# A decoder layer whose MLP runs as seven block products: where the weight sums are made, how the stages meet, and how the last chunk is done

## The chip, the cores and the metric

The kernel runs on one core of a Trainium2 chip. The metric is the device time of one execution in microseconds. The core has five engines that run their own instruction streams in order: TensorE (PE in the profile, its weight loads PEld), VectorE (DVE), ScalarE (ACT), GpSimd (POOL) and SyncE (SP). SP issues most transfers; GpSimd issues the transfers that add into their destination.

## The reference

One decoder layer on 512 tokens of width 2048, in float32: three mixers side by side, an output projection, and an MLP, then a last normalisation.

```python
def hybrid_layer(x, ...):
    h = rmsnorm(x, norm1_w)
    proj = h @ w_in
    ...
    y = jnp.concatenate([y_sb.astype(x.dtype), y_sc, y_gdn], axis=-1)
    x = x + y @ w_out
    h2 = rmsnorm(x, norm2_w)
    return x + jnp.square(jax.nn.relu(h2 @ w_up)) @ w_down
...
return rmsnorm(x, final_norm_w)
```

The change touches the MLP alone: `w_up` is 2048 x 8192, `w_down` 8192 x 2048.

## The kernel before

Every float32 operand of a large product is **split** into two fp32r parts, a rounded high part (a cast on ScalarE, L824) and the rest (a subtraction on VectorE, L825). A product is then three matmuls on TensorE (`mm3`, L108 to L112): high times high, high times low, low times high.

The MLP multiplies 2 x 2 block matrices with seven products in place of eight, numbered 1 to 7. Each product has one combination of weight blocks on one side and one of activation blocks on the other. The weight blocks are written `src(kh, d)`, and a **quarter** is one block of 128 x 1024 float32 (512 KB). The weight sides are: product 1 (0,0); 2 (1,0); 5 (0,0)+(0,1); 6 that plus (1,1); 3 (1,1); 4 the sum of all four; 7 (1,1)+(0,1). They are done in the order 1, 2, 5, 6, 3, 4, 7 (`PROD`).

`w_prep` (L831) makes the weight side of one product. At product 1 it loads three quarters on SP: `t` = (0,0), `v` = (1,0), `u` = (1,1). At product 5 and at product 7 a transfer issued by GpSimd adds (0,1) into `t` and into `u` (L835). At products 6 and 4 VectorE adds `u` and `v` into `t` (L836). Then the quarter is split into a tile `W`, of which there are three, used in turn: the split for a product can begin when the product three places before it is done with its tile. The quarters come from one ring of eight tiles.

Stages of the MLP, in the order of the program:

- **Up** (`up_pair`, L875): 32 groups. A group is seven products of 24 matmuls of 128 x 256 each, into PSUM tiles `pu`; 168 matmuls. ScalarE copies finished products out (L893), VectorE combines them (L897), applies relu and the norm factor (L920), ScalarE squares (L921), VectorE forms the activation sums for the next stage (L734, L738), and SP stores the 1 MB result `hs` to memory.
- **Down** (`unit`, L970): eight blocks (b) of two halves (j). One pair (b, j) is seven products of two chunks with 12 matmuls of 128 x 512 each, into `pp`; 168 matmuls. Activation tiles `A1` to `A7` are loaded from `hs` (`ha`) and split once per block. VectorE adds each product into the residual `xq` (L963, L966).
- The **last block** is cut: for both halves only half of its depth goes through the seven products, 84 matmuls each. The other half of its depth, for all columns, is done by plain products (`last`, L1032): 16 sums of 12 matmuls, 192 in all, after their weights `Wl` and activations `hl` have been split. Between them GpSimd multiplies by the final norm's weights (L1041).

Between the output projection (L767 to L794, 16 products of 48 matmuls over the tiles `big`) and the up stage lies a seam: the `mlp` pool with `q` and `W` takes over the memory of `big`. Group 0 there does products 1 and 2 up to their last step, and then the turn of the last block and the norm factor (`ending`). Between up and down lies another: the `A` tiles take over the memory of the up stage's activations.

Loads and splits carry a priority (`DPRIO`, `APRIO`): the scheduler puts them ahead of the code they are written in, some products early. That decides each engine's order.

## Time and profile before

| | us |
|---|---|
| median of 3 runs | 2417.95 (2413.97 to 2422.53) |
| the profiled execution | 2417.65 |
| its span in the trace | 2415.9 |

| stretch of the trace, us | what runs there |
|---|---|
| 0 to 912 | mixers and output projection |
| 912 to 932 | seam, with products 1 and 2 of group 0 |
| 932 to 1745 | the rest of the up stage |
| 1748 to 2357 | down stage by seven products |
| 2357 to 2408 | plain products of the last block |
| 2408 to 2416 | last norm and store |

The page's first part gives each engine's busy time. A row of a window gives, for one stretch, its length, the busy time of each engine with the number of instructions that began in it, the granted clock of TensorE, the share of the DMA engines' time in use and the rate. A row of the timeline has start, length, engine, line, operation, tile written and tiles read, a count if several are merged, and in brackets the idle time before it with what ended it. A row of the waits has who waited for whom, the total, the number of times and the longest. Up to 912 us the order of instructions on every engine is the same in both kernels, so the profile there holds for both.

### The profile page before, as it was taken

What the parts mean: (1) busy time and instruction counts of PE and PEld (TensorE: products, weight loads), DVE (VectorE), ACT (ScalarE), POOL (GpSimd) and SP (SyncE); (2) the same over time, 40 slices, a digit from 0 to 9 for tenths busy, and PEclk for the clock granted to TensorE, in tenths of its full rate; (3) what the DMA queues carried; (4) which work ended last, traced back from release to release, by engine and by line L of the source; (5) the groups of instructions that cost most, each with busy time, mean ns of one, the idle gap of its engine ahead of it and who ended that gap; (6) DMA issues with size and microseconds to landing.
All of it is one profiled execution on the core that took longest, in us unless ns stands there. A gap on an engine that the chain in (4) does not pass through costs nothing.

```text
span 2415.9 us, 33083 instructions
## 1 busy us (share of the span) xinstructions
PE 2245.7 (93%) x12698; PEld 1942.2 (80%) x12698; DVE 1656.8 (69%) x2320; ACT 1045.8 (43%) x1630; POOL 177.4 (7%) x235
## 2 busy tenths in 40 slices
PE   9999999999999998888888888988899999999987
PEld 8887787888888887888888788888777878777866
DVE  5799898646576555555555555565688988898875
ACT  5746554334445443333333333333344444444434
POOL 0000000000000110000000000000001010000003
PEclk9999999999999998999999999999999999999999
DMA  5322222232223445555555546555687675767542
GB/s 186 97 91 87 65 87 85 82 93 77 81 84 112 154 129 169 152 136 150 150 128 155 150 132 157 140 141 149 169 269 206 174 196 150 202 177 194 139 117 93
DMA packets 153582, 332.49 MB, mean 138 GB/s; under 512 B 19312, under 2 KB 60400, under 8 KB 153424
## 3 DMA queue, kind: packets, MB, share of 16 engines
q1 hardware_dynamic: 135568, 265.37, 32.6%
q0 software_dynamic: 17856, 65.02, 16.3%
q8 instruction: 99, 1.62, 0.3%
q14 instruction: 59, 0.48, 0.1%
HBM read 284.85 MB, written 45.48 MB: 137 GB/s over the span
## 4 chain that ended last, share of the span: by engine, by line
issue 55%; PE 34%; DVE 4%; POOL 2%; DMA 2%; ACT 1%; SPq 0%; POOLq 0%; ACTq 0%; DVEq 0%
PE mm L110 9%; PE mm L111 9%; PE mm L112 9%; POOL q L835 2%; DVE Yq L439 1%; PE mm L275 1%; PE mm L273 1%; PE mm L274 1%; DVE wlo L105 1%; DVE tq L437 1%; DMA q<-in_wd_dram 1%; DMA tmp<-x 0%; PE v L200 0%; PE v L201 0%; DVE W L825 0%
## 5 line engine op out<-in xcount | busy, mean ns | idle before, releaser
L824 ACT CAST W<-q 128x1024 fp32r<-128x1024 f32 x434 | 443.3, 1048 | 846.0 <-DMA q<-in_wu_dram 356.0
L825 DVE TENSOR_TENSOR W<-q,W 128x1024 fp32r<-128x1024 f32 x434 | 520.6, 1222 | 341.3 <-ACT W L824 340.4
L110 PE MATMUL mm<-big,whi 128*128 128x512 f32 x1024 | 406.1, 397 | 1.8 <-DVE tmp L558 1.6
L112 PE MATMUL mm<-big,wlo 128*128 128x512 f32 x1024 | 404.9, 396 | 0.0
L111 PE MATMUL mm<-big,whi 128*128 128x512 f32 x1024 | 404.8, 395 | 0.0
L110 PE MATMUL pu<-XS,W 128*128 128x256 f32 x1024 | 307.9, 301 | 62.6 <-ACT W L824 61.3
L110 PE MATMUL pp<-W,A 128*128 128x512 f32 x840 | 329.2, 395 | 16.3 <-ACT W L824 12.6
L112 PE MATMUL pu<-XS,W 128*128 128x256 f32 x1024 | 307.8, 301 | 36.2 <-DVE W L825 36.2
L111 PE MATMUL pp<-W,A 128*128 128x512 f32 x840 | 332.1, 395 | 5.0 <-DVE W L825 4.5
L112 PE MATMUL pp<-W,A 128*128 128x512 f32 x840 | 329.7, 393 | 1.0 <-DVE A L825 0.8
L111 PE MATMUL pu<-XS,W 128*128 128x256 f32 x1024 | 300.0, 293 | 0.0
L105 DVE TENSOR_TENSOR wlo<-raw,whi 128x512 fp32r<-128x512 f32 (+1 forms) x288 | 193.9, 675 | 147.0 <-ACT whi L104 133.3
L104 ACT CAST whi<-raw 128x512 fp32r<-128x512 f32 (+1 forms) x288 | 174.1, 606 | 267.0 <-PE mm L111 227.1
L110 PEld LDWEIGHTS pu<-XS,W 128*128 128x128 f32 x1024 | 205.7, 201 | 77.0 <-ACT W L824 76.4
L112 PEld LDWEIGHTS pu<-XS,W 128*128 128x128 f32 x1024 | 206.5, 202 | 46.7 <-DVE W L825 46.2
L110 PEld LDWEIGHTS mm<-big,whi 128*128 128x128 f32 x1024 | 193.9, 189 | 40.5 <-DVE tmp L558 1.8
L112 PEld LDWEIGHTS mm<-big,wlo 128*128 128x128 f32 x1024 | 193.8, 189 | 39.6
L111 PEld LDWEIGHTS mm<-big,whi 128*128 128x128 f32 x1024 | 193.7, 189 | 38.9 <-DVE big L723 0.3
L111 PEld LDWEIGHTS pu<-XS,W 128*128 128x128 f32 x1024 | 205.7, 201 | 0.0
L110 PEld LDWEIGHTS pp<-W,A 128*128 128x128 f32 x840 | 159.1, 189 | 57.3 <-ACT W L824 20.5
L111 PEld LDWEIGHTS pp<-W,A 128*128 128x128 f32 x840 | 159.1, 189 | 46.5 <-DVE W L825 12.3
L112 PEld LDWEIGHTS pp<-W,A 128*128 128x128 f32 x840 | 159.1, 189 | 34.2 <-DVE A L825 2.1
(289 smaller groups left out, 3459.5 us busy)
## 6 DMA issues: line engine op xcount, KB each, us to landing
q<-in_wd_dram SPq DMA_DIRECT2D x98, 512.0 KB
raw<-in_wa_dram SPq DMA_DIRECT2D x192, 256.0 KB
q<-in_wu_dram SPq DMA_DIRECT2D x96, 512.0 KB
q<-in_wu_dram POOLq DMA_DIRECT2D x64, 512.0 KB, 7.2
hs<-h SPq DMA_DIRECT2D x32, 1024.0 KB
q<-in_wd_dram POOLq DMA_DIRECT2D x60, 512.0 KB, 7.8
ha<-hs SPq DMA_DIRECT2D x49, 512.0 KB
raw<-in_wo_dram SPq DMA_DIRECT2D x64, 256.0 KB
```

The lines of the kernel that those rows point to most:

```text
L104: S.copy(out=hi[:, :n], in_=raw[:, :n])
L105: V.tensor_tensor(out=lo[:, :n], in0=raw[:, :n], in1=hi[:, :n].bitcast(F32), op=ALU.subtract)
L110: PE.matmul(p, lhsT=lh, rhs=rh, start=first, stop=False, skip_group_check=more)
L111: PE.matmul(p, lhsT=lh, rhs=rl, start=False, stop=False, skip_group_check=more)
L112: PE.matmul(p, lhsT=ll, rhs=rh, start=False, stop=last, skip_group_check=more)
L273: PE.matmul(o, lhsT=xw[k][:, 0, s], rhs=hi[:, ws], start=k == 0 and b % 2 == 0, stop=False)
L274: PE.matmul(o, lhsT=xw[k][:, 0, s], rhs=lo[:, ws], start=False, stop=False)
L275: PE.matmul(o, lhsT=xw[k][:, 1, s], rhs=hi[:, ws], start=False, stop=k == KT - 1 and b % 2 == 1)
L437: V.tensor_tensor(out=tv, in0=B[:, 0:i, i:i + 1].broadcast_to([16, i, n]), in1=Y[:, i:i + 1, i:32].broadcast_to([16, i, n]), op=ALU.mult)
L824: S.copy(out=o[:, 0], in_=src)
L825: V.tensor_tensor(out=o[:, 1], in0=src, in1=o[:, 0].bitcast(F32), op=ALU.subtract)
L835: more = lambda t, kh, d: nc.gpsimd.dma_start(out=t, in_=src(kh, d), accum_op=ALU.add)
```

## The change

It does these things:

1. All four quarters of a product set are loaded on SP: `t` (0,0), `v` (1,0), `x` (0,1), `u` (1,1), each from a ring of its own (three tiles for `t`, two for the others; nine tiles where there were eight).
2. Product 5's sum is made on VectorE from `x`. Straight after it, GpSimd begins a transfer that adds (1,1) into `x`; the result is the weight side of product 7.
3. In the up stage VectorE makes the sums of products 5, 6 and 4, and one adding transfer a group is left. In the down stage the order is 1, 2, 5, 6, 3, 7, 4 (`DOWN`); VectorE makes the sums of 5 and 6, and after the split for 6 a transfer adds (1,0) into `t` for product 4. Two adding transfers a chunk are left, as before.
4. Group 0's products 1 and 2 take their weights through the small tiles `whi` and `wlo` that served the output projection (`wload`), and six tiles of the `mlp` pool are allocated first (`ahead`).
5. `A1` of block 0 is loaded and split during the last up group, in tiles of the `mlp` pool.
6. The last block does half j = 0 in full by the seven products (168 matmuls) and half j = 1 in full by plain products (192 matmuls). The plain weights come through the same quarters; half of them are split into `W`, half into the tiles of `A5`, `A6`, `A3` and `A7`. The norm's work for half 0 lies beside the first 96 plain matmuls.

The number of matmuls in each stage stays the same.

```diff
-    PROD = (1, 2, 5, 6, 3, 4, 7)
+    UP = (1, 2, 5, 6, 3, 4, 7)
+    DOWN = (1, 2, 5, 6, 3, 7, 4)
...
+    def q_tile(tag):
+        return mlp.tile([P, 1024], F32, name="q", tag="q" + tag, bufs=3 if tag == "t" else 2)
+
+    def quarter(src, tag="t"):
+        q = ahead.pop(tag, None) or q_tile(tag)
         nc.sync.dma_start(out=q, in_=src)
         return q
...
+    def w_prep(n, st, src, down, split_too=True):
         with tc.high_priority(DPRIO):
-            more = lambda t, kh, d: nc.gpsimd.dma_start(out=t, in_=src(kh, d), accum_op=ALU.add)
-            more_on_v = lambda t, u: V.tensor_tensor(out=t, in0=t, in1=u, op=ALU.add)
+            on_v = lambda t, u: V.tensor_tensor(out=t, in0=t, in1=u, op=ALU.add)
             if n == 1:
-                st["t"] = quarter(src(0, 0))
-                st["v"] = quarter(src(1, 0))
-                st["u"] = quarter(src(1, 1))
+                for q, d in (("t", (0, 0)), ("v", (1, 0)), ("x", (0, 1)), ("u", (1, 1))):
+                    st[q] = quarter(src(*d), q)
             elif n == 5:
-                more(st["t"], 0, 1)
+                on_v(st["t"], st["x"])
+                nc.gpsimd.dma_start(out=st["x"], in_=src(1, 1), accum_op=ALU.add)
             elif n == 6:
-                more_on_v(st["t"], st["u"])
-            elif n == 4:
-                more_on_v(st["t"], st["v"])
-            elif n == 7:
-                more(st["u"], 0, 1)
-            o = mlp.tile([P, 2, 1024], F32R, name="W", tag="W", bufs=3, align_bytes=256)
-            split(o, st[{2: "v", 3: "u", 7: "u"}.get(n, "t")])
+                on_v(st["t"], st["u"])
+            elif n == 4 and not down:
+                on_v(st["t"], st["v"])
+            if not split_too:
+                return
+            o = ahead.pop("W", None) or w_tile()
+            split(o, st[{2: "v", 3: "u", 7: "x"}.get(n, "t")])
+            if n == 6 and down:
+                nc.gpsimd.dma_start(out=st["t"], in_=src(1, 0), accum_op=ALU.add)
...
+            Ws[n] = w_prep(n, st, lambda kh, d: wu[g, kh, d], False, g > 0 or n not in (1, 2))
+            if g == 0 and n in (1, 2):
+                Ws[n] = [wload(wu[0, n - 1, 0][:, 512 * c:512 * c + 512], 512) for c in range(2)]
...
     for g in range(FF // P // 2):
+        if g == FF // P // 2 - 1:
+            a_prep(0, 1, None)
         up_pair(g)
...
-        for j in range(2):
+        for j in range(2 if b < ND - 1 else 1):
...
+    def plain(c, d, kh):
+        q = quarter(wd[ND - 1, 1, kh, d][:, 1024 * c:1024 * (c + 1)], "txvu"[2 * d + kh])
+        if c == 0:
+            o = w_tile()
+        else:
+            n = (5, 6, 3, 7)[2 * d + kh]
+            o = dp.tile([P, 2, 1024], F32R, name=f"A{n}", tag=f"A{n}", bufs=1, align_bytes=256)
+        split(o, q)
+        return o
```

**VectorE in the up stage, around the start of a group.** Before, with `q_11518` as the group's `t`, `q_11520` its `v`, `q_11522` its `u`; `W_11524`, `W_11554`, `W_11584` belong to products 1, 2 and 5:

```order
L825 TENSOR_TENSOR W_11524<-q_11518,W_11524 128x1024
L825 TENSOR_TENSOR W_11554<-q_11520,W_11554 128x1024
L897 TENSOR_TENSOR raw_11289<-pu_11300,tmp_11474 128x256
L897 TENSOR_TENSOR raw_11290<-pu_11300,tmp_11385 128x256
L920 SCALAR_TENSOR_TENSOR raw_11289<-raw_11289,Rb_7222 128x512
L920 SCALAR_TENSOR_TENSOR raw_11290<-raw_11290,Rb_7222 128x512
L825 TENSOR_TENSOR W_11584<-q_11518,W_11584 128x1024
```

After, on the same engine at the same place, with `q_11560` as `t`, `q_11562` as `v`, `q_11564` as `x`; `W_11568`, `W_11598`, `W_11629` belong to products 1, 2 and 5:

```order
L825 TENSOR_TENSOR W_11568<-q_11560,W_11568 128x1024
L842 TENSOR_TENSOR q_11560<-q_11560,q_11564 128x1024
L825 TENSOR_TENSOR W_11598<-q_11562,W_11598 128x1024
L915 TENSOR_TENSOR raw_11329<-pu_11342,tmp_11517 128x256
L915 TENSOR_TENSOR raw_11330<-pu_11342,tmp_11428 128x256
L940 SCALAR_TENSOR_TENSOR raw_11329<-raw_11329,Rb_7222 128x512
L940 SCALAR_TENSOR_TENSOR raw_11330<-raw_11330,Rb_7222 128x512
L825 TENSOR_TENSOR W_11629<-q_11560,W_11629 128x1024
```

Product 5's sum stands on VectorE directly behind the split for product 1, and the adding transfer into `x` can begin from there.

**TensorE at the start of the up stage.** Before, the first matmuls behind the output projection (`W_8763` and `W_8788` are the split weights of products 1 and 2):

```order
L110 MATMUL pu_8766<-XP_7204,W_8763 128x256
L111 MATMUL pu_8766<-XP_7204,W_8763 128x256
L110 MATMUL pu_8791<-XP_7204,W_8788 128x256
L111 MATMUL pu_8791<-XP_7204,W_8788 128x256
L763 MATMUL pu_8823<-ident_78,tmp_8717 128x128 x4
L112 MATMUL pu_8766<-XP_7204,W_8763 128x256
```

After, at the same place (`whi` and `wlo` are the small tiles):

```order
L109 MATMUL pu_8779<-XP_7204,whi_8769 128x256
L110 MATMUL pu_8779<-XP_7204,whi_8769 128x256
L111 MATMUL pu_8779<-XP_7204,wlo_8770 128x256
L109 MATMUL pu_8779<-XP_7205,whi_8769 128x256
L110 MATMUL pu_8779<-XP_7205,whi_8769 128x256
L111 MATMUL pu_8779<-XP_7205,wlo_8770 128x256
```

Products 1 and 2 no longer read the `W` tiles, and the turn (L763) has moved behind all 48 of their matmuls.

**ScalarE at the end of the last block's seven products.** Before, the last two casts of `W` and what follows them (`hl` and `Wl` are the plain products' operands):

```order
L824 CAST W_19971<-q_19879 128x1024
L824 CAST W_19988<-q_19883 128x1024
L824 CAST hl_20011<-tmp_20009 128x512
L824 CAST hl_20016<-tmp_20014 128x512
L824 CAST hl_20021<-tmp_20019 128x512
L824 CAST hl_20026<-tmp_20024 128x512
L824 CAST Wl_20035<-q_20033 128x512
```

After (`W_20104` and `W_20119` are the two chunks of product 4, the last of the seven; `W_20146` and `W_20151` are the first plain weights; `A3_20312`, `A6_20307`, `A5_20302` and `A7_20317` are those of the second 96 plain matmuls):

```order
L824 CAST W_20104<-q_19860 128x1024
L824 CAST A3_20312<-q_20310 128x1024
L824 CAST A6_20307<-q_20305 128x1024
L824 CAST W_20119<-q_19883 128x1024
L824 CAST A5_20302<-q_20300 128x1024
L824 CAST W_20146<-q_20144 128x1024
L824 CAST A7_20317<-q_20315 128x1024
L824 CAST W_20151<-q_20149 128x1024
```

Three casts of weights that are used last now stand ahead of the last chunk of product 4 and of the first plain weights.

More of the change, by code (lines that the diff above doesn't have):

```diff
@@ L854, in h_tile @@
         return mlp.tile([P, 8, HT], F32, name="h", tag="h", bufs=2)
+    ahead = {}
+    for n in ("t", "v", "h", "W", "x", "u"):
+        ahead[n] = {"h": h_tile, "W": w_tile}.get(n, lambda: q_tile(n))()
     X4 = []
@@ L983, in unit @@
                     s = slice(i * P, (i + 1) * P)
[L984 to L985 removed]
+                    mm3(p[:, i], A[:, 0, k, s], A[:, 1, k, s], w[:, 0], w[:, 1], new and k == 0, k == HK - 1, not new)
+        for h, d in {1: ((0, 0),), 5: ((1, 1),), 6: ((0, 1),), 7: ((1, 0),)}.get(n, ()):
             x_load(h, d, j)
@@ L1009, in trunk @@
-    hl = []
-    for k in range(FBLK):
-        kh, sl = k // 2, HK // 2 + k % 2
-        t = tmp()
-        nc.sync.dma_start(out=t.rearrange("p (i t) -> p i t", i=2), in_=hs[ND - 1][:, 2 * kh:2 * kh + 2, sl])
-        o = fin.tile([P, 2, T], F32R, name="hl", tag="hl", bufs=FBLK, align_bytes=256)
-        split(o, t)
-        hl.append(o)
-    wfc = [fin.tile([P, 2, 512], F32, name=f"wf{d}") for d in range(2)]
-    for d in range(2):
-        nc.sync.dma_start(out=wfc[d], in_=wf[:, d * 1024:(d + 1) * 1024].rearrange("p (j f) -> p j f", j=2))
@@ L1020, in trunk @@
-    Wl = {}
-    for j in range(2):
-        for d in range(2):
-            for kh in range(2):
-                q = quarter(wd[ND - 1, j, kh, d][:, 1024:2048])
-                for k in range(2):
-                    o = fin.tile([P, 2, 512], F32R, name="Wl", tag="Wl", bufs=12, align_bytes=256)
-                    split(o, q[:, k * 512:(k + 1) * 512])
-                    Wl[j, d, kh * 2 + k] = o
+            for n in DOWN:
+                unit(b, j, n, dst)
+    with tc.high_priority(APRIO):
+        a_prep(ND - 1, 21, dp)
@@ L1045, in trunk @@
             for i in range(2):
-                last(0, d, h, i)
+                last(0, Wd, d, h, i)
+                norm_part(d, 0, h, i)
+    for d in range(2):
+        for kh in range(2):
+            Wd[d, kh] = plain(1, d, kh)
     for h in range(2):
```

85 lines of the change are left out of this document (48 added, 37 removed).

## The prediction

> **What bounds the kernel now.** I read the engines' busy times first, then the windows of the stretches that the change touches.
>
> ```profile
> span 2415.9 us, 33083 instructions
> PE 2245.7 (93%) x12698; PEld 1942.2 (80%) x12698; DVE 1656.8 (69%) x2320; ACT 1045.8 (43%) x1630; POOL 177.4 (7%) x235
> ...
> 912.40:931.55 19.15, 10.32 (x55) 9.20 (x55) 7.22 (x10) 7.73 (x11) 2.44 (x2) 0.73 0.90 304
> 931.55:1744.73 813.18, 703.05 (x5328) 672.36 (x5328) 467.06 (x603) 293.08 (x416) 56.51 (x65) 0.96 0.55 145
> 1748.44:2356.70 608.26, 589.72 (x2521) 474.22 (x2522) 514.59 (x452) 266.59 (x267) 50.46 (x58) 0.99 0.67 183
> 2356.70:2407.78 51.08, 45.75 (x192) 36.70 (x191) 29.05 (x46) 24.15 (x57) 19.16 (x15) 0.97 0.20 77
> ```
>
> TensorE is busy 93% of the span, but the records of its matmuls overlap, so the number to use is the stride between two starts. It comes from stretches without a wait:
>
> ```profile
> 1302.06 0.28 PE L111 MATMUL pu<-wlo,W 128*128 128x256 f32 x1
> 1304.34 0.28 PE L112 MATMUL pu<-whi,W 128*128 128x256 f32 x1
> ...
> 2106.29 0.39 PE L112 MATMUL pp<-W,A 128*128 128x512 f32 x1
> 2117.85 0.39 PE L112 MATMUL pp<-W,A 128*128 128x512 f32 x1
> ```
>
> In the up stage 19 strides take 2.28 us, 0.120 each; with a second stretch at 0.118 I use **0.1195**. In the down stage 51 strides take 11.56 us, **0.2267**. Without waits, then, the rest of the up stage would take 5328 x 0.1195 = 636.7 us where it takes 813.2: 176.5 us are lost, 5.5 in each of 32 groups. The down stage would take 2520 x 0.2267 = 571.3 where it takes 608.3, and the plain products 192 x 0.2267 = 43.5 where they take 51.1. The up stage is the place to look at. Its waits and one group show what ends last:
>
> ```profile
> POOL q L835 <- DVE W L825: 770.1, 65, 17.2
> ACT W L824 <- DMA q<-in_wu_dram: 356.0, 59, 8.0
> ...
> L824 ACT CAST W<-q x206: 1038/1054/1060, 1754.8 to 2345.3; 128x1024 fp32r<-128x1024 f32 x103
> L825 DVE TENSOR_TENSOR W<-q,W x206: 1214/1220/1227, 1756.1 to 2346.4; 128x1024 fp32r<-128x1024 f32 x103
> ...
> 1297.52 0.86 POOL L835 DMA_DIRECT2D q<-in_wu_dram  x1 [13.68 <-DVE W L825]
> 1305.04 2.94 ACT L824 CAST W<-q 128x1024 fp32r<-128x1024 f32 x3 [5.38 <-DMA q<-in_wu_dram]
> 1306.12 3.50 DVE L825 TENSOR_TENSOR W<-q,W 128x1024 fp32r<-128x1024 f32 x3 [3.83 <-ACT W L824]
> 1306.14 0.38 PE L110 MATMUL pu<-XS,W 128*128 128x256 f32 x1 [1.52 <-ACT W L824]
> 1307.73 0.42 PE L110 MATMUL pu<-XS,W 128*128 128x256 f32 x1
> 1310.51 0.41 PE L111 MATMUL pu<-XS,W 128*128 128x256 f32 x1
> 1310.92 0.28 PE L110 MATMUL pu<-XS,W 128*128 128x256 f32 x1
> ```
>
> GpSimd waits for a split to be done with a quarter, begins the adding transfer at 1297.5, ScalarE waits until 1305.0 for it to land, casts, and TensorE, which ran out of products 1.52 us before, starts at 1306.1. It then runs slow until 1310.9: at 1307.7 the stride is some 0.21, so about 16 matmuls lose 1.5 us more. The chain is issue 0.9, landing 7, cast 1.05, and ahead of it a split that waits for a tile of `W`. It runs twice a group, for products 5 and 7. Products that cost 24 x 0.1195 = 2.87 us each don't cover it.
>
> **The change, part by part.**
>
> *Up stage.* Product 5's sum goes to VectorE: 1.22 us, once in 32 groups, 39 us more; the adding transfer for it goes (32), a load on SP comes (32). With two tiles for `x` that load is begun a group ahead, about 20 us. The other transfer now starts behind product 5's sum, which stands right behind the split for 1. That split can begin when product 3 is done: cast 1.05, split 1.22, sum 1.22, issue 0.86, landing 7.2 make 11.6 us. Its result is first wanted by the cast for product 7, whose tile comes free when product 6 ends, six products or 17.2 us after product 3. So 5.6 us are left; at the longest landing of the stage some 0:
>
> ```profile
>   DMA to landing us min/median/max: 5.4/7.2/12.9
> ```
>
> What is late next? VectorE: 467.06 us in 5328/168 = 31.7 groups, 14.7 a group, with the sum 15.9 of 20.1. ScalarE: 293.08/31.7 = 9.2. DMA: a group now uses 0.55 x 25.4 = 14 us; by the queues
>
> ```profile
> q1 hardware_dynamic: 135568, 265.37, 32.6%
> q0 software_dynamic: 17856, 65.02, 16.3%
> ```
>
> a MB costs 0.163 x 2415.9/65.02 = 6.06 us as an adding transfer and 2.97 as a load, so half a MB moved from one to the other makes 14 - 3.0 + 1.5 = 12.5 of 20.1. Nothing is above 80%, so TensorE sets the end: 20.1 us a group, plus 0.2 a group for an odd late split (bounds 0 and 2.0, the latter a wait of 0.6 with the slow stretch of 1.5 behind it, once a group; I take nearly the lower since the smallest reserve that I find by following VectorE's order through a group at these durations is 1.9 us). 636.7 + 6 - 813.2 = **-170.5**.
>
> *The first seam.*
>
> ```profile
> 912.49 0.69 DVE L776 TENSOR_TENSOR tmp<-mm,xr 128x512 f32<-128x512 f32 x1 [7.67 <-PE mm L112]
> 917.70 1.23 DVE L731 TENSOR_TENSOR XS<-xsum,XS 128x1024 fp32r<-128x1024 f32 x1 [1.11 <-ACT XS L730]
> 918.67 0.58 PE L110 MATMUL pu<-XP,W 128*128 128x256 f32 x1 [6.27 <-ACT W L824]
> 931.55 0.39 PE L110 MATMUL pu<-XS,W 128*128 128x256 f32 x1 [2.41 <-ACT W L824]
> ```
>
> TensorE stops at 912.4 for 6.27 us, since `q` and `W` lie where `big` lay and are loaded and split only then; product 5 starts at 931.55. Now products 1 and 2 read small tiles that don't wait for `big`: 42 matmuls run from 912.4 on, 5 us. Product 5 needs `XS`, which ends at 918.9, the turn, and its own sum, cast and first split, about 2.6: 921.5. If the loads, which still can't start before `big` is free, land at 913 + 8, it is 913 + 8 + 1.2 + 1.05 + 1.2 = 924.5 or later. Bounds 918.9 and 926; I take the nearer row, `XS`: **-10**.
>
> *The second seam.*
>
> ```profile
> 1741.22 1.37 SPq L958 DMA_DIRECT2D ha<-hs  x3
> 1744.45 0.28 PE L112 MATMUL pu<-XS,W 128*128 128x256 f32 x1
> 1748.44 0.80 PE L110 MATMUL pp<-W,A 128*128 128x512 f32 x1 [3.71 <-ACT A L824]
> ```
>
> `A1` is loaded while the last group still runs, so the wait of 3.7 for its cast goes; a second of restart and `A2`'s load stay: I take 2 (0 to 3.7). **-1.7**.
>
> *Down stage.* Product 5's sum moves to VectorE, product 4's moves to a transfer: still four additions a pair there, still four adding transfers, and two more loads of 512 KB, 3 us of DMA time in 38. Late casts after transfers cost TensorE 37 us in 15 pairs' worth of products. Two changes cut this: product 5 needs no transfer, and product 4, now last, leaves its transfer product 3 and product 7 (2 x 5.44 = 10.9 us) to land in. But VectorE stands at 514.6/608.3 = 85%, at 88 to 90% when the stage is denser, and DMA goes from 0.67 to about 0.77. Each chunk's transfer frees `t` late: with three tiles, its next load has about a chunk, 2.7 us, to spare. I leave half a microsecond in each of 15 pairs, 8 us (bounds 0 and all of the 37). At the end of block 7 three casts of late plain weights stand ahead of the last chunk of product 4; their quarters wait for tiles, so ScalarE may stand in front of them for about 2 us and TensorE with it, near the row of the same place now:
>
> ```profile
> 2326.42 0.49 PE L110 MATMUL pp<-W,A 128*128 128x512 f32 x1 [2.18 <-ACT W L824]
> ```
>
> With the slow stretch I price it at 4. 571.3 + 8 + 4 - 608.3 = **-25.0**.
>
> *Plain products.* Now they start behind a wait of 5 us for the split of `Wl`:
>
> ```profile
> 2362.14 0.77 PE L111 MATMUL mm<-Wl,hl 128*128 128x512 f32 x1 [5.00 <-DVE Wl L825]
> ...
> 2374.51 1.29 POOL L1041 TENSOR_TENSOR xq<-xq,wf 128x512 f32<-128x512 f32 x1 [1.74 <-ACT tmp L1040]
> 2374.97 1.38 DVE L825 TENSOR_TENSOR Wl<-q,Wl 128x512 fp32r<-128x512 f32 x1 [0.44 <-ACT Wl L824]
> ```
>
> The activations are split already in the changed kernel, and its first weights use tiles of `W` that turn over during product 4. 43.5 + 1 - 51.1 = **-6.6** (bounds 0 and -7.6). The last norm, 8.1 us, stays. The row of 1.38 us is a split beside a product on GpSimd, where the operation of the same size at 912.49 took 0.69; the eight products for half 0 now lie beside splits as well, 8 x 0.7 = 5.6 us of VectorE in 23 us of matmuls, which hides them. The Trainium skill ("SBUF — State Buffer", section "Who interferes with whom") has a rule on it: a VectorE operation with two inputs in SBUF contends with a GpSimd instruction that reads SBUF, and the later one is held up. The doubled row agrees; by it the longest delay of one split is GpSimd's 1.29 us, which would cost up to 1.3 us where the first plain weights wait, and nothing in the sum is changed by it.
>
> **The sum.** -10 - 170.5 - 1.7 - 25.0 - 6.6 = -213.8, against the execution that was profiled, 2417.65 us (the span of 2415.9 and 1.75 around it): **2204 us**. The median shown, 2417.95, differs by 0.3. Less than 0.3%, 7 us, can't be told from no change here.
>
> **The rivals.**
>
> *A new wait in the up stage (A).* The splits come in one order on two engines that don't look ahead; a late cast for any of seven products would stop TensorE once a group, 0.6 of wait and 1.5 of slow stretch. For it: the shortest reserve is 1.9 us, and landings reach 12.9. Against: loads are begun 20 us ahead. 32 x 2 = 64: **2268**.
>
> *The down stage stays as bound as now (B).* VectorE at nearly 90% and DMA at 0.77 delay a load per chunk: all 25 us but a few stay, plus a cost of the third `t`'s late load. +28: **2232**.
>
> *The slow stretches stay (C).* The granted clock of the up stage is 0.96, and what I call slow restarts may come from something else than the waits; 32 x 1.5 = 48 then stay: **2252**. The Trainium skill speaks for it ("TensorE: Matmul & The Clock Gate", section "Why this matters for your kernels"): only idle gaps above about 3 us bring the clock down, so gaps of 1.52 wouldn't be the cause. The trace differs: a slow stretch stands right behind the gap of 1.52, and the long stretch 1850 to 2250 of the down stage, whose gaps are at most 0.8, has a clock of 1.00:
>
> ```profile
> 1850.00:2250.00 400.00, 394.47 (x1716) 320.02 (x1716) 347.17 (x302) 181.40 (x179) 36.54 (x42) 1.00 0.67 179
> ...
> PE pp L110 <- ACT W L824: 4.1, 8, 0.8
> ```
>
> *It doesn't do what it says (D).* If another chain in the up stage is as long as the one that goes, only the other terms are left, 43 us: **2374**. Against it: every wait of TensorE there is for a `W` that an adding transfer feeds.
>
> *Slower (E).* Product 5's sum now stands on VectorE at the head of everything else: behind it the split for 2, the taking of products, relu and the split for 5. If the load of `x` is late, all of this stops, and TensorE with it. The gain, 213.8/32 = 6.7 us a group, is used up when TensorE waits that long in each, that is when a load begun 20.1 us ahead, with the reserve of 1.9, takes some 29 us. The longest landing of an adding transfer is 12.9, at a DMA share of 0.55, and the first seam ran at 0.90. At 8 us late a group, 32 x 8 - 214 = +42: **2460**.
>
> **How the numbers follow.** Forecast 0.76, A 0.10, B 0.08, C 0.02, D 0.02, E 0.02. The forecast's own bounds are 2183 (no loss left in the up and down stages but the 4 at its end, the first seam at 918.9, nothing at the second) and about 2217 (seam at 926, the 8 in the down stage doubled). The range 2183 to 2268 takes in A, B and C and leaves D and E out. Faster by over 0.3%: all but E, with a little for what I don't see, 0.97; within 0.01; slower 0.02.
>
> **What would show it.** In the changed kernel: groups of the up stage 20.1 to 20.5 us apart at a granted clock of 1.00, ScalarE's wait for `in_wu` transfers nearly gone (the step on the chain); else A, with TensorE waiting for a `W` whose quarter came from SP. Product 5 of group 0 at 919 to 926. No wait for `A` at the second seam. VectorE at 88 to 90% in the down stage and TensorE's strides at 38.5 us a pair; a wait at product 4's last chunk and the first plain weights of 2 us. The prediction is wrong if landings of `x` grow past 17 us in the up stage, or if VectorE, not TensorE, turns out to be the engine that is waited for.

## The result, and the profile after

| | before | changed |
|---|---|---|
| median, us | 2417.95 | 2195.19 (2192.34 to 2196.6) |
| the profiled execution's span, us | 2415.9 | 2193.2 |
| ratio, 95% interval | | 0.9075 (0.906 to 0.9091) |

The kernel is 222.8 us faster; 213.8 were forecast. The page of the changed kernel, its first part and the two largest groups of its fifth (count, busy time and mean of one, then the idle time ahead of them and what ended most of it):

```profile
span 2193.2 us, 33146 instructions
PE 2153.2 (98%) x12698; PEld 1893.1 (86%) x12698; DVE 1695.1 (77%) x2335; ACT 1067.3 (49%) x1621; POOL 150.4 (7%) x203
...
L824 ACT CAST W<-q 128x1024 fp32r<-128x1024 f32 x436 | 455.0, 1051 | 563.4 <-PE pp L111 247.1
L825 DVE TENSOR_TENSOR W<-q,W 128x1024 fp32r<-128x1024 f32 x436 | 530.5, 1225 | 121.6 <-ACT W L824 121.0
```

What ended most of ScalarE's waits ahead of a cast of `W` was a transfer (356 us, in the up stage); over the whole changed kernel it is TensorE, at the tiles `pp` of the down stage (247 of 563 us). In the up stage, between 950 and 1550 us, its waits ahead of a cast are these (who waited for whom, total, times, longest):

```profile
ACT W L824 <- DVE q L842: 89.5, 60, 2.1
ACT W L824 <- issue: 87.3, 61, 1.5
ACT W L824 <- PE pu L111: 70.9, 60, 2.0
```

No transfer is among the first five. Casts now wait for VectorE's sums or for a tile that TensorE still reads, and since TensorE is busy throughout, these waits cost nothing. The same stretches as before, by the windows of the changed kernel (length, busy time of each engine, granted clock, DMA share, rate), from the last matmul of the output projection on:

```profile
907.34:916.34 9.00, 7.46 (x56) 6.41 (x54) 6.62 (x10) 5.25 (x9) 1.95 (x2) 1.00 0.68 229
916.34:1555.37 639.03, 635.55 (x5329) 634.53 (x5329) 510.51 (x636) 313.97 (x419) 28.32 (x33) 1.00 0.65 188
1555.37:2138.61 583.24, 575.54 (x2523) 473.24 (x2521) 518.59 (x453) 279.80 (x276) 55.14 (x61) 1.00 0.76 222
2138.61:2184.72 46.11, 44.26 (x193) 35.62 (x191) 22.67 (x31) 16.47 (x40) 16.14 (x13) 1.00 0.15 57
```

Beside the stretches of before, each from the first matmul of one to the first of the next:

| stretch | before, us | changed, us | difference | forecast |
|---|---|---|---|---|
| up to the end of the output projection | 912.2 | 907.3 | -4.9 | 0 |
| seam, to the first matmul of product 5 | 19.3 | 9.0 | -10.3 | -10 |
| up stage and second seam | 816.9 | 639.0 | -177.9 | -172.2 |
| down stage | 608.1 | 583.2 | -24.9 | -25.0 |
| plain products and end | 59.4 | 54.6 | -4.8 | -6.6 |

The first row is no effect of the change: the order of instructions there is the same, and of the kernels below, e1, with the seam of before, starts its last matmul of the projection at 906.85 and e9, with the changed seam, at 911.56. Executions differ there by some 5 us.

### The profile page after: what moved, and what is told of

It reads as the page before. It is cut to its first block, busy times and chain, and to the rows that moved or that the text cites. A ratio compares the mean times of both kernels' runs of the same rounds, so it can differ in the third digit from the quotient of the medians.

```text
span 2193.2 us, 33146 instructions
## 1 busy us (share of the span) xinstructions
PE 2153.2 (98%) x12698; PEld 1893.1 (86%) x12698; DVE 1695.1 (77%) x2335; ACT 1067.3 (49%) x1621; POOL 150.4 (7%) x203
## 3 DMA queue, kind: packets, MB, share of 16 engines
q8 instruction: 99, 1.62, 0.3%
## 4 chain that ended last, share of the span: by engine, by line
PE 91%; DVE 5%; DMA 1%; ACT 1%; issue 1%; SPq 0%; ACTq 0%; DVEq 0%
PE mm L110 10%; PE mm L109 10%; PE mm L111 10%; PE pu L111 10%; PE pu L109 10%; PE pu L110 10%; PE pp L110 8%; PE pp L111 8%; PE pp L109 8%; DVE wlo L104 1%; PE mm L274 1%; PE mm L272 1%; PE mm L273 1%; DVE W L825 1%; DVE Yq L438 1%
## 5 line engine op out<-in xcount | busy, mean ns | idle before, releaser
L824 ACT CAST W<-q 128x1024 fp32r<-128x1024 f32 x436 | 455.0, 1051 | 563.4 <-PE pp L111 247.1
L825 DVE TENSOR_TENSOR W<-q,W 128x1024 fp32r<-128x1024 f32 x436 | 530.5, 1225 | 121.6 <-ACT W L824 121.0
L110 PE MATMUL pp<-W,A 128*128 128x512 f32 x840 | 328.0, 390 | 3.9 <-DVE W L825 3.9
L111 PE MATMUL pp<-W,A 128*128 128x512 f32 x840 | 327.4, 390 | 1.1 <-DVE A L825 1.1
L109 PE MATMUL pp<-W,A 128*128 128x512 f32 x840 | 325.6, 391 | 2.8 <-ACT A L824 2.8
L111 PE MATMUL pu<-XS,W 128*128 128x256 f32 x1024 | 288.9, 282 | 1.2 <-DVE W L825 1.2
L109 PE MATMUL pu<-XS,W 128*128 128x256 f32 x1024 | 289.0, 282 | 1.0 <-ACT W L824 0.8
L110 PE MATMUL pu<-XS,W 128*128 128x256 f32 x1024 | 288.6, 282 | 0.0
L109 PEld LDWEIGHTS pu<-XS,W 128*128 128x128 f32 x1024 | 193.4, 189 | 2.0 <-ACT W L824 1.6
L111 PEld LDWEIGHTS pu<-XS,W 128*128 128x128 f32 x1024 | 193.4, 189 | 1.7 <-DVE W L825 1.7
L110 PEld LDWEIGHTS pu<-XS,W 128*128 128x128 f32 x1024 | 193.3, 189 | 0.0
L842 DVE TENSOR_TENSOR q<-q 128x1024 f32<-128x1024 f32 x156 | 190.2, 1219 | 2.1 <-DMA q<-in_wd_dram 0.7
L110 PEld LDWEIGHTS pp<-W,A 128*128 128x128 f32 x840 | 158.1, 188 | 38.4 <-DVE W L825 5.6
L109 PEld LDWEIGHTS pp<-W,A 128*128 128x128 f32 x840 | 158.0, 188 | 37.3 <-ACT A L824 4.1
```

The costliest lines, as they stand in the source:

```text
L109: PE.matmul(p, lhsT=lh, rhs=rh, start=first, stop=False, skip_group_check=more)
L110: PE.matmul(p, lhsT=lh, rhs=rl, start=False, stop=False, skip_group_check=more)
L111: PE.matmul(p, lhsT=ll, rhs=rh, start=False, stop=last, skip_group_check=more)
L824: S.copy(out=o[:, 0], in_=src)
L825: V.tensor_tensor(out=o[:, 1], in0=src, in1=o[:, 0].bitcast(F32), op=ALU.subtract)
L842: on_v = lambda t, u: V.tensor_tensor(out=t, in0=t, in1=u, op=ALU.add)
```

## The experiments

Twelve kernels ran, each against runs of the kernel before on the same chip. The length of a group in the up stage is read from one stretch of the windows, 1000 to 1500 us, in which every kernel is within that stage. These are its rows for before, the changed kernel and e5:

```profile
1000.00:1500.00 500.00, 432.13 (x3287) 413.47 (x3287) 287.47 (x376) 178.82 (x255) 33.92 (x39) 0.96 0.55 143
```

```profile
1000.00:1500.00 500.00, 500.00 (x4213) 500.00 (x4212) 400.13 (x503) 244.31 (x325) 21.72 (x25) 1.00 0.64 185
```

```profile
1000.00:1500.00 500.00, 435.23 (x3340) 413.14 (x3340) 291.58 (x376) 183.51 (x259) 34.92 (x40) 0.98 0.58 159
```

500 us hold 3287 matmuls before and 4213 after; at 168 a group that is 25.56 and 19.94 us. For all kernels (the last column is empty where the run changes something other than the sums of the up stage, and for e12, which has the changed ones):

| kernel | median, us | ratio (95% interval) | group in the up stage, us |
|---|---|---|---|
| before | 2417.95 | 1 | 25.56 |
| changed | 2195.19 | 0.9075 (0.906 to 0.9091) | 19.94 |
| e1, only the up stage's sum | 2232.66 | 0.925 (0.922 to 0.9279) | 19.93 |
| e2, product 7 as before | 2251.79 | 0.9334 (0.9309 to 0.9358) | 21.72 |
| e3, product 5 by a transfer | 2233.33 | 0.9255 (0.923 to 0.928) | 20.93 |
| e4, all sums on VectorE | 2196.58 | 0.9101 (0.9072 to 0.9129) | 19.93 |
| e5, 5 and 7 as before | 2364.78 | 0.9786 (0.9752 to 0.982) | 25.15 |
| e6, before with four `W` | 2400.05 | 0.9931 (0.9906 to 0.9956) | 25.38 |
| e7, first seam through `W` | 2198.27 | 0.9092 (0.9053 to 0.9132) | |
| e8, nothing allocated ahead | 2194.06 | 0.9075 (0.9035 to 0.9115) | |
| e9, down sums as before | 2205.82 | 0.9125 (0.9107 to 0.9143) | |
| e10, down sums on VectorE | 2203.55 | 0.9122 (0.9105 to 0.9138) | |
| e11, second seam as before | 2196.7 | 0.9091 (0.907 to 0.9112) | |
| e12, before with the sums of both stages | 2212.23 | 0.9158 (0.9139 to 0.9177) | |

### Which part carries the up stage: e1

```diff
 # the kernel before; up is true in the up stage
+                if up:
+                    st["x"] = quarter(src(0, 1))
                 st["u"] = quarter(src(1, 1))
+            elif n == 5 and up:
+                more_on_v(st["t"], st["x"])
+                more(st["x"], 1, 1)
             elif n == 5:
                 more(st["t"], 0, 1)
...
-            elif n == 7:
+            elif n == 7 and not up:
                 more(st["u"], 0, 1)
...
-            split(o, st[{2: "v", 3: "u", 7: "u"}.get(n, "t")])
+            split(o, st[{2: "v", 3: "u", 7: "x" if up else "u"}.get(n, "t")])
```

> The kernel before with one part of the change: in the up stage (0,1) is loaded on SP, product 5's sum is made on VectorE and the transfer that adds (1,1) into it is begun there; the ring of eight quarters, both seams, the down stage and the last block stay. Theory (the chain split, adding transfer, cast sets the up stage): 170 to 178 us of the gain come, 2240 to 2250. Rival (the nine tiles in rings of their own let loads start earlier, and that is the gain): under 40 us, 2380 or more. Rival (new seams and last block carry more than 43 us): 2260 to 2300.

These few lines bring the group to 19.93 us, that of the changed kernel, with the old ring of eight quarters. The rings of their own are not the gain. At 2232.7 the kernel is somewhat below what the theory gave; its runs reach from 2225 to 2237.

### Each chain alone: e2, e3 and e4

In e2 product 7's sum is made as before, in the up stage alone:

```diff
-                nc.gpsimd.dma_start(out=st["x"], in_=src(1, 1), accum_op=ALU.add)
+                if down:
+                    nc.gpsimd.dma_start(out=st["x"], in_=src(1, 1), accum_op=ALU.add)
...
+            elif n == 7 and not down:
+                nc.gpsimd.dma_start(out=st["u"], in_=src(0, 1), accum_op=ALU.add)
...
-            split(o, st[{2: "v", 3: "u", 7: "x"}.get(n, "t")])
+            split(o, st[{2: "v", 3: "u", 7: "x" if down else "u"}.get(n, "t")])
```

> The changed kernel, but in the up stage product 7's side is made as before: a transfer adds (0,1) into u once the split for 3 is done with u. Product 5's sum stays on VectorE, all rings stay. Theory: that chain is 1.05 + 1.22 + 0.86 + 7.2 + 1.05 = 11.4 us behind the end of product 2, and products 5, 6, 3, 4 cover 11.5, so about every second landing is late: 1 to 2.7 us a group with the slow stretch, 32 to 86 us, 2227 to 2281; the granted clock of the up stage falls to 0.97 to 0.99. Rival (where the transfer starts doesn't matter, only that a sum left GpSimd's queue): 2195 within 5.

In e3 product 5's sum is a transfer:

```diff
-                on_v(st["t"], st["x"])
+                if down:
+                    on_v(st["t"], st["x"])
+                else:
+                    nc.gpsimd.dma_start(out=st["t"], in_=src(0, 1), accum_op=ALU.add)
                 nc.gpsimd.dma_start(out=st["x"], in_=src(1, 1), accum_op=ALU.add)
```

> The changed kernel, but in the up stage a transfer adds (0,1) into t for product 5 once the split for 1 is done, in place of VectorE's sum; the transfer for product 7 still starts early into x. Theory: the chain for 5 is 11.4 us as well against 11.5 of products 4, 7, 1, 2: 2227 to 2281, by the wait of TensorE for product 5's W. Rival (rings and earlier loads are the gain): 2195 within 5. If e2 and e3 cost 86 each, the two chains' shares are equal and add up to the 178 of the up stage.

And in e4 VectorE makes the last sum too:

```diff
-                nc.gpsimd.dma_start(out=st["x"], in_=src(1, 1), accum_op=ALU.add)
+                if down:
+                    nc.gpsimd.dma_start(out=st["x"], in_=src(1, 1), accum_op=ALU.add)
...
+            elif n == 7 and not down:
+                on_v(st["x"], st["u"])
```

> The changed kernel, but in the up stage product 7's sum too is made on VectorE, from x and u; no adding transfer is left there. VectorE then needs 15.9 + 1.2 = 17.1 of 20.1 us a group. Theory (TensorE sets the pace as long as no engine is full, reserves of 1.9 us hold): 2195 within 5. Rival (VectorE's order has no reserve left, it becomes the bound before it is full): one late split a group, 32 x 1 to 2 us, 2227 to 2260.

e2 and e3 cost 57 and 38 us by their medians, inside what was expected; the group is 1.8 and 1.0 us longer. e4 costs nothing that can be told (its interval overlaps the changed kernel's), with VectorE at 427 of 500 us. So where the sum of product 7 is made doesn't matter, as long as it isn't late, and VectorE at 85% is no bound. But 1.8 and 1.0 together are half of the 5.6 us a group that went. Something ties the two chains, and it isn't that two adding transfers run in one group: e3 has two as well, at a DMA share of 0.74, and its group is 20.93 us.

### The loop: e5 and e6

One group of the kernel before, in the timelines of GpSimd, ScalarE and VectorE. The rows go on from those of 1297.52 and 1305.04 in the prediction:

```profile
1308.89 0.88 POOL L835 DMA_DIRECT2D q<-in_wu_dram  x1 [10.50 <-DVE W L825]
1322.53 0.88 POOL L835 DMA_DIRECT2D q<-in_wu_dram  x1 [12.76 <-DVE W L825]
...
1314.46 1.05 ACT L824 CAST W<-q 128x1024 fp32r<-128x1024 f32 x1 [6.21 <-PE pu L112]
1318.67 2.00 ACT L824 CAST W<-q 128x1024 fp32r<-128x1024 f32 x2 [1.85 <-DVE q L836]
...
1315.55 1.23 DVE L825 TENSOR_TENSOR W<-q,W 128x1024 fp32r<-128x1024 f32 x1 [1.69 <-ACT W L824]
1317.36 1.22 DVE L836 TENSOR_TENSOR q<-q 128x1024 f32<-128x1024 f32 x1
1319.76 2.36 DVE L825 TENSOR_TENSOR W<-q,W 128x1024 fp32r<-128x1024 f32 x2 [0.17 <-ACT W L824]
```

Read it as a ring, in which each step waits for the one before and the last one lets the first begin again. At 1297.52 GpSimd begins the transfer for product 7. ScalarE stands in front of its cast until 1305.04; the casts for products 1 and 2 of the next group have stood behind it and run with it (the three that the row counts). The split for 1 is done at 1308.4, and only then, at 1308.89, the transfer for product 5 can begin, since it adds into the tile that was split. Its cast runs at 1314.46; behind it come VectorE's sum for 6, the casts for 6 and 3, and their subtractions, until 1322.12. The split for 3 lets the next transfer for 7 begin at 1322.53. The half turns are 11.4 and 13.6 us, a turn 25.0; the mean group is 25.56. TensorE is in it at most where one row says so (the cast at 1314.46, ended by TensorE by the trace). There too the transfer is the likelier end: it was begun at 1308.89 and its landing takes 5.4 us or more, while product 7, whose tile of `W` that cast takes, starts its last matmul at 1311.51. e5 puts both old chains into the changed kernel (the edits of e2 and e3 together), e6 gives the kernel before a fourth tile of `W` and, for the room, two quarters less:

```diff
 # e6, the kernel before
-QB = 8
+QB = 6
...
-            o = mlp.tile([P, 2, 1024], F32R, name="W", tag="W", bufs=3, align_bytes=256)
+            o = mlp.tile([P, 2, 1024], F32R, name="W", tag="W", bufs=4, align_bytes=256)
```

> The changed kernel with the edits of e2 and e3 together: in the up stage both products 5 and 7 get their sums by a transfer as before, rings and loads stay (x is loaded there but not read). e2 cost 57 us and e3 38. Theory of a loop: in the kernel before, the cast for 5 waits on ScalarE for its transfer, the casts for 6 and 3 stand behind it, and only the split for 3 lets the transfer for 7 begin, whose cast in turn stands ahead of those for 1 and 2; a turn is two times (0.86 issue, 7.2 landing, three casts 2.94, the last subtraction 1.2) = 24.4 us, near the 25.4 a group that was seen, and TensorE has no part in it. Each of e2 and e3 opened that loop. Then together they cost far more than the sum: 32 x (25.0 to 25.4 - 20.0) = 160 to 173, 2355 to 2368. Rival (each transfer is late by itself, against the products that cover it): the costs add, 2195 + 57 + 38 = 2290. Rival (the rings carry part of the gain): under 2270.

> The kernel before with four tiles of W in place of three, and six quarters in place of eight for the room. A split can then begin one product (2.87 us in the up stage) sooner. Theory of the loop (ScalarE's order and the landings, not the tiles of W, set the group): within 20 us of before, 2395 to 2435. Rival (a transfer is late because the split ahead of it waits for a tile of W): most of the 5.5 us a group goes, 2250 to 2320. Rival (six quarters are too few, loads come late): over 2440.

e5 is at 2364.8, where the ring gives 2355 to 2368 and the sum of the two costs 2290. e6 gains 0.7%, of 9% to be had. The waits of ScalarE and GpSimd in e6, between 950 and 1620 us (who waited for whom, total, times, longest), show the ring running on with the spare tile. A wait is 6.0 and 11.8 us on average, the same as before (356.0 in 59 and 770.1 in 65):

```profile
ACT W L824 <- DMA q<-in_wu_dram: 310.4, 52, 7.3
...
POOL q L835 <- DVE W L825: 626.5, 53, 13.8
```

Changing either chain alone opens the ring, and leaves only the lateness of the other. That the costs don't add up is shown by e2, e3 and e5; that the link is the order of ScalarE's casts is read from the rows, and no run changed this order by itself. In the changed kernel nothing of it is left; one group there, GpSimd, then ScalarE and VectorE behind product 3:

```profile
1214.51 0.87 POOL L848 DMA_DIRECT2D q<-in_wu_dram  x1 [19.08 <-ACT W L824]
...
1213.35 1.05 ACT L824 CAST W<-q 128x1024 fp32r<-128x1024 f32 x1 [2.00 <-PE pu L111]
...
1211.39 1.23 DVE L825 TENSOR_TENSOR W<-q,W 128x1024 fp32r<-128x1024 f32 x1 [0.63 <-ACT W L824]
1212.65 1.23 DVE L842 TENSOR_TENSOR q<-q 128x1024 f32<-128x1024 f32 x1
```

The sum for 5 (1212.65) follows the split for 1 directly, GpSimd's transfer starts 0.63 us after its end (the trace puts its wait down to the cast beside it, which ends later), and that cast has waited for TensorE.

### The first seam: e7 and e8

e7 leaves out the small tiles for products 1 and 2, e8 empties the list of tiles allocated ahead:

```diff
 # e7
-            Ws[n] = w_prep(n, st, lambda kh, d: wu[g, kh, d], False, g > 0 or n not in (1, 2))
-            if g == 0 and n in (1, 2):
-                Ws[n] = [wload(wu[0, n - 1, 0][:, 512 * c:512 * c + 512], 512) for c in range(2)]
+            Ws[n] = w_prep(n, st, lambda kh, d: wu[g, kh, d], False)
 # e8
-    for n in ("t", "v", "h", "W", "x", "u"):
+    for n in ():
```

> The changed kernel, but products 1 and 2 of group 0 take their weights through W again; the six tiles are still allocated first. Changed kernel: product 5 starts 9.0 us behind the last matmul of the output projection (19.3 before). Theory (the small tiles carry the seam): 17 to 20 us, 2203 to 2206 in all. Rival (the early allocation carries it): 9 to 12 us.

> The changed kernel, but no tile of the mlp pool is allocated ahead; group 0's products 1 and 2 still take the small tiles. Theory (the small tiles carry the seam): 9 to 11 us from the last matmul of the output projection to product 5. Rival (the order of allocation decides which part of the output projection's memory the first quarter waits for): 12 to 17 us.

In e7 product 5 starts 16.4 us behind the projection (9.0 in the changed kernel), in e8 9.0. So the small tiles carry 7.4 us of the seam, and the early allocation does nothing that can be seen. The other 3 of the 10.3 us aren't theirs: e1 and e6, which have the old seam, both take 16.4 us, where the profiled execution of before took 19.3; why it did is open. But e7's time rises by 3 us only, where I expected 8 to 11. From the projection's last matmul to the up stage's last it needs 651.9 us, the changed kernel 648.1, and e1, which has the old seam, 649.6. The rest of the 7 us is given back within group 0. The windows of the changed kernel show where:

```profile
915.00:925.00 10.00, 7.05 (x50) 5.87 (x48) 6.91 (x8) 5.76 (x8) 1.00 (x1) 1.00 1.04 327
925.00:935.00 10.00, 8.92 (x60) 8.73 (x61) 6.99 (x9) 5.04 (x9) 0.00 (x0) 0.83 0.58 220
```

The DMA engines are full from 915 to 925, and TensorE, now early, begins 50 matmuls where some 84 fit. Its waits between 915 and 927 us are for splits, and by the trace the casts of `W` at 915.24, 918.84 and 923.50 waited for VectorE's sums. So the making of group 0's operands sets the pace there; whether their loads or the chain of sum, cast and split is what holds it isn't shown.

### The down stage and the second seam: e9 to e12

e9 puts the sums and the order of the down stage back (transfers for 5 and 7, order 3, 4, 7), e10 leaves one transfer there and gives product 4's sum to VectorE:

```diff
 # both
-    DOWN = (1, 2, 5, 6, 3, 7, 4)
+    DOWN = (1, 2, 5, 6, 3, 4, 7)
...
-            elif n == 4 and not down:
+            elif n == 4:
                 on_v(st["t"], st["v"])
...
-            if n == 6 and down:
-                nc.gpsimd.dma_start(out=st["t"], in_=src(1, 0), accum_op=ALU.add)
...
 # e9 alone
+                if down:
+                    nc.gpsimd.dma_start(out=st["t"], in_=src(0, 1), accum_op=ALU.add)
...
+            elif n == 7 and down:
+                nc.gpsimd.dma_start(out=st["u"], in_=src(0, 1), accum_op=ALU.add)
...
```

> The changed kernel with the down stage's weight sums and order of products as before (transfers for 5 and 7, VectorE for 6 and 4, order 3, 4, 7, no load of x); seams, up stage and last block stay as changed. Theory (the sums' place is most of the 25 us won in the down stage: 400/1716 x 168 = 39.2 us a pair against 400/1766 x 168 = 38.1 now): 15 x 1.1 = 17 us more, 2207 to 2217, with waits of TensorE for W spread over the blocks. Rival (the gain of the down stage lies in its start and in the last block): 2195 within 4. Rival (the loop of the up stage closes here too, with two chunks a product): over 2225.

> The changed kernel, but in the down stage the order is 1, 2, 5, 6, 3, 4, 7 and VectorE also makes the sum for product 4, so that one adding transfer a chunk is left (as in the up stage). VectorE: 518.6 + 30 x 1.22 = 555 us of 583, 95%, 37.0 of 38.1 in a pair. Theory (below 100% TensorE still sets the pace, as e4 showed at 85%): 2195 within 6. Rival (at 95% its in-order queue makes splits late): 0.5 to 2 us a pair, 2203 to 2230.

e11 loads `A1` after the up stage again (without the call in front of the last group):

```diff
-        if g == FF // P // 2 - 1:
-            a_prep(0, 1, None)
...
-        if j == 0 and b + n > 1:
+        if j == 0:
```

> The changed kernel, but A1 of block 0 is loaded and split after the up stage's pools are closed, as before. Theory: the wait of 3.7 us for the cast of A1 comes back between the last matmul of the up stage and the first of the down stage, and 3 to 5 us in the time, 2198 to 2201. Rival (TensorE only waits for A2 a little earlier): the wait comes back and the time stays within 1.5.

e12 gives the kernel before all the sums and the order, and none of the other parts:

```diff
 # the kernel before; both stages
-                st["t"] = quarter(src(0, 0))
-                st["v"] = quarter(src(1, 0))
-                st["u"] = quarter(src(1, 1))
+                for q, d in (("t", (0, 0)), ("v", (1, 0)), ("x", (0, 1)), ("u", (1, 1))):
+                    st[q] = quarter(src(*d), q)
             elif n == 5:
-                more(st["t"], 0, 1)
+                more_on_v(st["t"], st["x"])
+                more(st["x"], 1, 1)
...
-            elif n == 7:
-                more(st["u"], 0, 1)
...
+            if n == 6 and down:
+                more(st["t"], 1, 0)
...
```

> The kernel before with the sums of the changed kernel in both stages (four loads, nine tiles in rings, product 5 on VectorE, transfers begun ahead, order 3, 7, 4 in the down stage); both seams and the last block as before. Without a wait the down stage would be 571 us; before it lost 7.5 in its first 85 us, 11.2 in the middle, 17.0 in the last block. Theory (the sums clear the middle, the last block's own form the rest): middle 0 to 1, last block 13 to 18, and against e1 (2232.7, where only the up stage has its sum) 7 to 12 us less: 2221 to 2226. Rival (the sums' place clears the last block too): last block under 5, 2207 to 2213. Rival (the last block in one chunk with products of 12 matmuls gives the longer chain no room): last block over 20, 2228 or more.

The windows of the down stage, cut into its first 85 us, the next 400, and the rest with the last block, for before, the changed kernel, e9 and e12:

```profile
1748.44:1833.44 85.00, 82.79 (x342) 65.44 (x343) 71.80 (x65) 40.25 (x40) 6.10 (x7) 0.96 0.87 272
1833.44:2233.44 400.00, 394.12 (x1714) 319.37 (x1713) 346.80 (x302) 181.79 (x179) 35.67 (x41) 1.00 0.68 180
2233.44:2356.52 123.08, 112.63 (x468) 89.25 (x468) 96.00 (x87) 44.55 (x49) 8.69 (x10) 0.97 0.52 130
```

```profile
1555.37:1640.37 85.00, 78.50 (x333) 62.54 (x332) 73.45 (x69) 41.61 (x42) 6.11 (x7) 0.98 0.94 305
1640.37:2040.37 400.00, 400.00 (x1767) 331.23 (x1766) 360.58 (x313) 188.95 (x183) 38.28 (x44) 1.00 0.75 212
2040.37:2138.61 98.24, 97.05 (x427) 79.47 (x425) 84.55 (x73) 49.24 (x51) 10.76 (x10) 1.00 0.68 192
```

```profile
1558.27:1643.27 85.00, 81.94 (x352) 66.33 (x351) 75.39 (x71) 44.02 (x45) 7.43 (x9) 0.98 0.89 279
1643.27:2043.27 400.00, 393.75 (x1714) 319.62 (x1712) 347.58 (x303) 180.79 (x177) 35.19 (x41) 1.00 0.69 182
2043.27:2148.90 105.63, 102.89 (x449) 83.60 (x447) 92.91 (x80) 51.19 (x54) 13.56 (x12) 1.00 0.58 155
```

```profile
1648.20:2048.20 400.00, 400.00 (x1767) 331.20 (x1766) 359.12 (x311) 188.22 (x183) 37.45 (x43) 1.00 0.75 210
2048.20:2152.60 104.40, 97.17 (x412) 78.45 (x411) 83.50 (x76) 39.54 (x44) 6.97 (x8) 0.97 0.61 169
```

The time that a stretch lost is its length less its matmuls by 0.2267 us (good to about 1 us). Start, middle and end lost 7.5, 11.4 and 17.0 us before, and 9.5, about 0 and 1.4 in the changed kernel.

- The middle is the doing of the sums with their order of products: e9, with the old ones, loses 11.4 there again, e12, with the new ones in the kernel before, nothing. e9's time is 11 us up, just under what was expected, but not by the middle alone: beside the changed kernel it loses 2.4 more at the end and 4.3 less at the start, 9.5 in all.
- The end is for the larger part the last block's form: e12, with the old form and the new sums, loses 11.0 there of 17.0; e9, with the new form and the old sums, 3.8. My theory for e12 had 13 to 18 there, and 2221 to 2226 in all; it came to 2212, the time of its first rival, whose loss of under 5 in the last block didn't come. The sums help the last block more than I gave them, but they don't clear it: the largest wait of TensorE left there in e12, 4.3 us, is for a cast of `W` for product 4, whose sum is now a transfer.
- In the start the changed kernel loses 2 us more than before, at a DMA share of 0.94. e9, with the same seam and the old sums, loses 5.2 there at 0.89. So the new sums, with the loads that they bring, cost some 4 us at the start of this kernel's stage. With the old seam they cost less (e12 loses 6.6 there, e1 with the old sums 5.9); why was not tried.
- e10 has one transfer a chunk and VectorE at 94% (374.7 of 400 us in the middle), and is 8 to 11 us slower than the changed kernel (by the medians and by the ratios, whose intervals don't touch). TensorE's waits between 1643 and 2043 us are all for a cast:

```profile
PE pp L109 <- ACT W L824: 5.7, 6, 1.0
```

The changed kernel has no wait of TensorE between 1640 and 2040 us at all. All six stand at product 2 of a block's first half, where six of e9's nine waits stand too, with VectorE at 87%. The down stage of e10 is 5.6 us longer than the changed kernel's; another 4.3 lie behind it, where TensorE waits 4.0 us for VectorE's addition into `xq`. e10 differs from the changed kernel in the order of the products as well as in the place of one sum, so what a VectorE at 94% costs by itself isn't shown.

- In e11 the wait for `A1` is back:

```profile
1558.73 0.50 PE L109 MATMUL pp<-W,A 128*128 128x512 f32 x1 [4.25 <-ACT A L824]
```

From the last matmul of the up stage to the end e11 takes 641.3 us, the changed kernel 637.95: 3.4 us, as the theory has it. The medians, 1.5 apart, can't tell it.

## Why the prediction was right, and where its steps were off

**The forecast case came**: TensorE paces the up stage, at 19.94 us a group where I had 20.1 + 0.2. The 6 us that I left for late splits weren't needed: the stage took 639.0 where 5328 strides make 636.7. None of the rivals came. The forecast was 8.8 us above the result; 4.9 of this is the stretch ahead of the MLP, where two executions of the same instructions differ.

**What bounded the up stage before** was the step that named the wrong tie. The prediction said that each chain starts behind a split that waits for a tile of `W` and isn't covered by the products beside it. By e6 the tile isn't it: a spare one brings 0.2 us a group. The two transfers hold each other, by the rows through ScalarE's order, and the ring of 25 us that they make sets the group; e2, e3 and e5 show that they are tied (1.8 and 1.0 us a group alone, 5.2 together). The reading under D, that every wait of TensorE in the up stage is for a `W` fed by an adding transfer, misses this too: at 1307.08 TensorE waits 0.45 us for product 1, whose quarter SP loads; its cast stood behind that for 7. The sum was right although this step wasn't, and in that it was lucky, because the step after it, the new transfer begun behind the split for 1 with 5.6 us to spare, opens this ring as well. That later step was worked out and held: the landings are 5.5 at the median and the row of GpSimd above stands where that step puts it.

**The first seam** was right at its place, 10.3 for 10, though the small tiles made only 7.4 of it, and wrong in what it is worth: 7 us earlier against e7 became 3 to 4 at the end of the stage. I bounded when product 5 can start, and didn't ask what bounds group 0 behind it. This loss lies within the up stage's row of the table.

**The second seam** was worth 3.4 (e11) where I took 1.7; what I left for `A2` wasn't lost at the seam, but is part of the 9.5 us at the start of the down stage, where I had nothing of its own; TensorE's waits for `A` tiles there come to 3.9.

**The down stage's** sum was right, 24.9 for 25.0, and its parts weren't. I spread the 37 us lost evenly over 15 pairs and left half a microsecond in each. In fact 17 of them were lost at the end, nearly all in the cut last block; the middle's 11 went to nothing, and the start got 2 worse. That the total came out within 0.1 is luck. The wait at the end of block 7 was there, smaller than the 4 I priced; the rows of TensorE in the changed kernel:

```profile
2135.98 0.50 PE L110 MATMUL pp<-W,A 128*128 128x512 f32 x1 [0.95 <-DVE W L825]
2140.51 0.50 PE L110 MATMUL mm<-W,A 128*128 128x512 f32 x1 [1.29 <-DVE W L825]
```

They stand at the last chunk of product 4 and at the first plain products, the two places named; the second one and what follows it make the plain products' gain smaller than forecast. Which cast causes it was not tried.

**The slow stretches** (rival C) went with the waits: the clock of the up stage is 1.00, and 0.98 again in e5. I set this against the Trainium skill's rule of idle gaps above about 3 us ("TensorE: Matmul & The Clock Gate", section "Why this matters for your kernels"), on one gap of 1.52 us. The rows of before speak less against the rule than I wrote: behind that gap only two matmuls ran until 1307.08, so that TensorE stood nearly idle for 2.5 us before the slow stretch. The granted clock over the next 4 us was 0.57:

```profile
1304.00:1307.00 3.00, 1.12 (x8) 0.71 (x6) 0.89 (x1) 1.96 (x3) 0.00 (x0) 1.00 0.52 202
1307.00:1311.00 4.00, 3.92 (x19) 3.90 (x20) 2.61 (x3) 1.25 (x3) 0.88 (x1) 0.57 0.54 143
```

Nor does a slow stretch stand behind every such gap, as I had priced it: a group earlier TensorE waits 1.62 us at 1280.23 and 0.45 at 1281.18, and the clock over the 4 us from there is 1.00. What decides between the two isn't shown. The lower bound of the forecast, 2183, is 2 us less than its own terms make.

## What to carry to other kernels

When two slow steps are issued on engines that work in order, look whether each stands ahead of what the other needs to start. Then they make a ring whose turn is the period. A spare buffer brought only 0.2 us a group here, and half of a repair hides what the other half is worth: opening the ring at one place brought 4.6 or 3.8 us a group, at both 5.6. And before pricing a loss as so much per unit, cut the stage into start, middle and end.

## What I hadn't expected of the hardware

Adding transfers of 512 KB take 5.3, 5.5 and 6.8 us to land (least, median, most) in the up stage of the changed kernel, with one a group, and 5.5, 6.6 and 9.4 in e5 with two, at DMA shares of 0.64 and 0.58. Neither their number nor the share of the DMA engines tells it: e2, with one a group at 0.56, has 6.2, 6.7 and 9.2, and e3, with two at 0.74, 5.4, 5.7 and 6.8. What e2 and e5 have in common is the transfer for product 7 begun behind the split for 3; why it lands later is open. And TensorE kept its stride of 0.119 us in e4 with VectorE at 85% of the time: an in-order engine that is that full cost nothing there.
